# Output projection of a hybrid decoder layer: eight block products replaced by seven, with the operand sums made in the stage before

## The chip, the cores and the metric

The kernel runs on one core of one Trainium2 chip. The metric is the device time of one execution in microseconds (us). The kernel before took 1744.45 us, the median of three runs (1742.46 to 1744.65).

The core's engines work side by side: TensorE (PE in the profile; its weight loads are PEld) multiplies matrices, VectorE (DVE), ScalarE (ACT) and GpSimd (POOL) work elementwise, and SyncE's queue (SP) issues nearly all transfers between the main memory (DRAM) and the on-chip memory. Each engine takes its instructions in a fixed order and waits where an input is not there yet.

## The reference

One layer of a decoder for 1024 prompt tokens and 8 single sample tokens, in 32-bit floats, model width 1024. What matters here:

```python
x = x + jnp.concatenate([o_a, y], axis=-1) @ w['w_out']      # (tokens, 2048) @ (2048, 1024), plus the residual
h = rmsnorm(x, w['norm2_w'])
gate, val = jnp.split(h @ w['w_up'], 2, axis=-1)             # 1024 -> 2 x 2816
gate, buf_f_new = causal_dwconv(gate, buf_f, w['ffn_conv_w'], w['ffn_conv_b'])
x = x + (jax.nn.silu(gate) * val) @ w['w_down']
```

`o_a` (1024 wide) comes from eight heads of a gated recurrence (HGRN2), `y` (1024 wide) from the Mamba-2 mixer. Both are fed by one input projection. A final RMSNorm follows.

## The kernel before

All tokens (1032 with the samples) are processed together, with features on the 128 partitions and tokens along the free dimension. A product in 32-bit precision is made of three matmuls in the rounded format float32r: high x high, high x low and low x high. So every operand is first *split*: ACT casts it to its high part, DVE subtracts this from the original for the low part.

Order of the work:

- **Input projection and mixers** (to about 824 us). `in_job` makes one 128-wide output tile with 3 token chunks x 8 x 3 = 72 matmuls. The mixers' own work, `ssd` and `head(h)`, is interleaved by `drive`, which lets so many matmuls of the queue of jobs go by for each piece of the head. The heads' outputs and `y` are stored as 16 row tiles of 128 x 1032 in DRAM (`mix_d`; rows 0 to 7 from the heads, 8 to 15 from the mixer).
- **Output projection**, jobs a, b, c, d. The tokens are cut in two groups of 516 (`hf`), the inner dimension in the mixer's half (`r0 == 8`) and the heads' half (`r0 == 0`). a and b make the first group, c and d the second. Each of these has eight output tiles `m`, and each tile two column quarters of 258 tokens with 24 matmuls each. `mix_rows` loads eight row tiles of a half and splits them (L1107 to L1110). `Weight` loads 512 KB of `w_out` for a tile, and `round` splits it (L1093, L1094). Products of a and c are copied out of PSUM by ACT (L1166), those of b and d added by DVE (L1168). `residual` transposes a tile of the input x on TensorE (L852, L854) and adds it (L847). `final` stores the tile to `x1_d` (L1179) and collects squares for the norm (L1182 to L1186).
- **Token sets** `set_of(i)` for each group i: `norm` multiplies by the norm (L1326); then seven operands p1 to p7 of a seven-product block form are made of the four blocks a1, b1, a2, b2 (inner half 1 or 2, first or second 258 columns), by differences and sums (L1342, L1354), and split (L1336, L1337, L1355, L1358). The first group's set is made during c and d, the second group's during d and the first up group.
- **Up projection** in 22 groups `ups(j, seq)`. Each multiplies the seven token operands of both groups with seven weight operands: 14 x 12 = 168 matmuls of 258 columns. `up_sums` builds the weight sums on POOL (L1423), `up_split` splits them (L1444 to L1447). The down projection's weight sums are made ahead by `down_sums`, on POOL and by way of DRAM (`wsum_d`; L1203, L1206).
- **Down projection**, also as seven products, whose token operands (`at`) come back from DRAM (`act_d`). `last_step` starts its loads and splits in the last up group. `fin` makes the output.

What sets the order: the list of jobs, each with its run-ahead `load`; `after(n, f)`, which issues f after n more matmuls; `spread(pieces, n)`, which issues one piece every n matmuls; and for TensorE the order written by hand. On the other engines a planner orders the instructions by its estimates, bound by edges as in `behind` (an instruction of ACT goes behind the marked one).

The lines of the core loop and of the boundary to the up projection:

```python
hi, lo = mixes[r0, hf]
for c in cols:
    ps = psmm.tile([P, 512], F32, tag="mm", name=nm("mm"))[:, :QW]
    yield from steps(w.parts, 0, P, hi, lo, cs, ps)          # 8 rows x 3 matmuls
    ...
finish("d10")
after(22, lambda: set_norm(1, 1))
after(24, lambda: spread(second, 1))
for _ in ups(0, [(name, i) for i in range(2) for name in FIRST]):
    tick()
```

## Time and profile before

| | |
|---|---|
| median of the runs | 1744.45 us |
| the profiled execution, its own time | 1741.85 us |
| its span, first to last instruction | 1740.1 us |
| TensorE busy | 98% of the span |
| DVE, ACT, POOL busy | 68%, 48%, 29% |
| mean transfer rate | 138 GB/s |
| output projection, first to last matmul | 823.7 to 1045.0 us |
| up projection begins | 1045.0 us |
| down projection begins | 1496.7 us |

How to read it: a line of the profile names the source line, engine and operation, what it writes and reads, the shape and the count; after the bar stand the busy time in us, the mean of one in ns, and the idle time of the engine just before, with what ended it. Matmuls overlap, so their mean length is longer than the distance from one to the next.

### The profile page before, as it was taken

How to read it: one execution, taken by the hardware profiler on the slowest of the kernel's cores; microseconds unless marked ns; L12 is line 12 of the kernel's file. 1: busy time of each engine (PE TensorE's matmuls, PEld its weight loads, DVE VectorE, ACT ScalarE, POOL GpSimd, SP SyncE). 2: the span in 40 equal slices, each digit the busy share in tenths (PEclk: the TensorE clock that was granted, in tenths of full speed). 3: DMA queues.
4: the chain of work that ended last, by engine and by line, in shares of the span. 5: the costliest groups of instructions: out<-in, count | busy, mean ns of one | idle time of the engine just before them, and what ended most of it. 6: DMA issues, size and time to landing. Idle time of an engine off the chain costs nothing. (4 is left out here: it accounts for less than half of the span.)

```text
span 1740.1 us, 39019 instructions
## 1 busy us (share of the span) xinstructions
PE 1704.3 (98%) x15967; PEld 1650.9 (95%) x15967; DVE 1177.9 (68%) x2053; ACT 838.8 (48%) x1507; POOL 506.2 (29%) x500
## 2 busy tenths in 40 slices
PE   7999999999999999999999999999999999999998
PEld 7999998999999999999999998999999999999998
DVE  4657888568555654665666678877787777775664
ACT  6478688443543444444344444343433343444344
POOL 1102242112211210110112124776667775000001
PEclk9999999999999999999999999999999999999999
DMA  5123474564232322233556451445555543786463
GB/s 158 37 79 97 140 210 141 154 173 131 76 104 65 86 81 82 87 93 94 179 176 202 116 143 59 147 142 151 148 162 165 153 140 117 250 267 229 152 190 124
DMA packets 319689, 239.31 MB, mean 138 GB/s; under 512 B 18380, under 2 KB 287734, under 8 KB 319494
## 3 DMA queue, kind: packets, MB, share of 16 engines
q1 hardware_dynamic: 319222, 236.72, 45.4%
q8 instruction: 125, 2.05, 0.5%
q14 instruction: 54, 0.44, 0.1%
q0 software_dynamic: 288, 0.10, 0.0%
HBM read 178.18 MB, written 58.77 MB: 136 GB/s over the span
## 5 line engine op out<-in xcount | busy, mean ns | idle before, releaser
L94 PE MATMUL mm<-hh,wh 128*128 128x344 f32 x1248 | 406.4, 326 | 0.0
L94 PE MATMUL mm<-hl,wh 128*128 128x344 f32 x1248 | 403.7, 323 | 0.0
L94 PE MATMUL mm<-hh,wl 128*128 128x344 f32 x1248 | 402.4, 322 | 0.0
L94 PEld LDWEIGHTS mm<-hh,wh 128*128 128x128 f32 x1248 | 234.7, 188 | 2.9 <-issue 0.9
L94 PEld LDWEIGHTS mm<-hl,wh 128*128 128x128 f32 x1248 | 234.8, 188 | 2.2 <-issue 0.9
L94 PEld LDWEIGHTS mm<-hh,wl 128*128 128x128 f32 x1248 | 234.9, 188 | 2.0 <-issue 1.0
L94 PE MATMUL ub<-uh,wh 128*128 128x258 f32 x704 | 199.5, 283 | 2.1 <-DVE fext L1497 1.6
L94 PE MATMUL ub<-ul,wh 128*128 128x258 f32 x704 | 199.9, 284 | 1.5 <-DVE ul L1358 1.5
L94 PE MATMUL ub<-uh,wl 128*128 128x258 f32 x704 | 199.0, 283 | 0.0
L94 PE MATMUL mm<-mx,wh 128*128 128x258 f32 x1024 | 190.9, 286 | 1.6 <-DVE mx L1110 1.1
L94 PE MATMUL dn<-at,wh 128*128 128x260 f32 (+1 forms) x896 | 163.0, 282 | 0.0
L94 PEld LDWEIGHTS mm<-mx,wh 128*128 128x128 f32 x1024 | 158.5, 189 | 3.3 <-DVE mx L1110 1.6
L94 PE MATMUL ua<-uh,wh 128*128 128x258 f32 x528 | 150.1, 284 | 0.5 <-ACT us L1469 0.5
L94 PE MATMUL ua<-ul,wh 128*128 128x258 f32 x528 | 149.9, 284 | 0.0
L94 PE MATMUL ua<-uh,wl 128*128 128x258 f32 x528 | 149.4, 283 | 0.0
L94 PE MATMUL mm<-mx,wl 128*128 128x258 f32 x512 | 145.3, 284 | 1.7 <-DVE wl L1094 1.7
L94 PEld LDWEIGHTS dn<-at,wh 128*128 128x128 f32 x896 | 137.6, 188 | 0.0
L94 PEld LDWEIGHTS ub<-uh,wh 128*128 128x128 f32 x704 | 133.0, 189 | 2.5 <-ACT uh L1336 1.8
L94 PEld LDWEIGHTS ub<-ul,wh 128*128 128x128 f32 x704 | 133.4, 189 | 1.9 <-DVE ul L1358 1.9
L94 PEld LDWEIGHTS ub<-uh,wl 128*128 128x128 f32 x704 | 133.4, 190 | 0.0
L94 PE MATMUL dn<-at,wl 128*128 128x260 f32 (+1 forms) x448 | 126.6, 283 | 3.9 <-DVE wl L1613 3.9
L1447 DVE TENSOR_TENSOR wl<-wt,wh 128x512 fp32r<-128x512 f32 x88 | 89.5, 1036 | 58.3 <-ACT wh L1446 58.3
(342 smaller groups left out, 3726.9 us busy)
## 6 DMA issues: line engine op xcount, KB each, us to landing
ws<-in_w_in_dram SPq DMA_DIRECT2D x52, 512.0 KB
ws<-in_w_up_dram SPq DMA_DIRECT2D x44, 512.0 KB
at<-act_d SPq DMA_DIRECT2D x77, 258.0 KB
ws<-in_w_out_dram SPq DMA_DIRECT2D x36, 512.0 KB
wq<-in_w_down_dram SPq DMA_DIRECT2D x44, 256.0 KB
wsum_d<-wq SPq DMA_DIRECT2D x22, 512.0 KB
mx<-mix_d SPq DMA_DIRECT2D x32, 258.0 KB
csb<-cs_d SPq DMA_DIRECT2D x32, 256.0 KB
```

The lines of the kernel that those rows point to most:

```text
L94: PE.matmul(out, lhsT, rhs, start=start, stop=stop)
L1447: V.tensor_tensor(lo[:, cs], sums[name], hi[:, cs].bitcast(F32), op=ALU.subtract)
```

## The change

The output projection is written as a seven-product block form, too: the inner dimension has two halves (mixer, heads), the tokens of each group two column halves, and the output width two halves. With y0, y1 the mixer's rows and o0, o1 the heads' rows (first and second 258 columns of a group), the row operands are: p1 y0; p7 y0 - y1; p4 o1; p6 (y1 - o1) - y0; p5 y1 - o1; p2 o0; p3 o0 + p6.

- The jobs are p1, p7, p4, p6, p5, p2, p3. Each covers both token groups, has four output tiles (half the width) and 4 x 2 x 24 matmuls; p3 does group 0 for all four tiles and then group 1 with the same weights kept. Each needs its own eight row tiles.
- `row_sums`, new at the end of each head, loads the mixer's row tile (into the head's k buffer), makes the four sums on POOL and stores them to `row_d`; for the last head p7's row is not stored but subtracted on DVE when it is split.
- `out_sums` makes the weight sums for p6, p5, p4 and p7 from 16 groups on POOL and stores them to `wo_d`. It runs in the heads, ahead of the first four groups of `down_sums`, with one piece every 10 matmuls instead of every 70, and four pieces between a group's load and its sums.
- `out_add`: p1 and p7 are copied out of PSUM by ACT; p4, p6 and p5 are added or subtracted on DVE, with one more operation on POOL for p6 and p5; p2 and p3 are added on DVE. The second column halves are final after p5, the first after p2 (lower half of the width) and p3 (upper half).
- The residual is loaded in pieces of 258 tokens x 256 columns, two pieces ahead, and added during the products p6, p5 and p2.
- The token sets of both groups are made in two parts, `second_halves` (from p2 on) and `first_halves` (group 0 from p3b on, group 1 in the first up group). The norm's column multiplication goes to ACT, the multiplication by the row norm to DVE, on two tiles at once. DVE splits and set operations are now bound behind the last marked DVE eviction (`vbehind`).
- The first up group multiplies p5 and p4 of both groups first, then the other five of group 0 and of group 1.
- `last_step` opens and loads the first tiles of the down projection earlier and splits them in smaller pieces.

```diff
+    def residual_load(i, c, q):
+        t0, cols = (2 * i + c) * QW, slice(2 * q * P, (2 * q + 2) * P)
+        xs, xd = tl("t", "xs")[:, :512], tl("us", "xd")
+        if t0 + QW <= T:
+            fetch(xs.rearrange("p (b m) -> p b m", b=2), x_prompt[0, t0:t0 + 256, cols].rearrange("(b p) m -> p b m", p=P))
+            fetch(xd[:2, :256], x_prompt[0, t0 + 256:t0 + QW, cols])
         else:
+            n = T - t0 - P
+            fetch(xs[:, :256], x_prompt[0, t0:t0 + P, cols])
+            fetch(xs[:n, 256:], x_prompt[0, t0 + P:T, cols])
+            fetch(xd[:ND, :256], x_sample[:, 0, cols])
         return xs, xd
...
+    def residual(i, c, q, xs, xd):
+
+        n, nd = (P, 2) if (2 * i + c + 1) * QW <= T else (T - (2 * i + c) * QW - P, ND)
+        ps, pd = bank("xtp"), bank("xtd", "nx")
+        for m in range(2):
+            ms = slice(m * P, (m + 1) * P)
+            PE.transpose(ps[:, m * 256:m * 256 + P], xs[:, ms], ident)
+            PE.transpose(ps[:, m * 256 + P:m * 256 + P + n], xs[:n, 256 + m * P:256 + (m + 1) * P], ident[:n, :n])
+            PE.transpose(pd[:, m * 8:m * 8 + nd], xd[:nd, ms], ident[:nd, :nd])
...
+    def residuals(items):
+        loads = [residual_load(*it) for it in items[:2]]
+        for n, it in enumerate(items):
+            yield
+            if n + 2 < len(items):
+                loads.append(residual_load(*items[n + 2]))
+            residual(*it, *loads[n])
...
+        fetch(k[:, :NT], mix_d[8 + h])
...
+        spread(row_sums(h, k, sg), 14)
+
+    def halves(t):
+        return t.rearrange("p (i c t) -> p i c t", i=2, c=2)
+
+    ROWS = ("p7", "p5", "p6", "p3")
+    MID = 2 * QW
+    row_d = dram.tile([4, 8, P, MID], F32, name="row_d")
+
+    def row_sums(h, k, sg):
+        a, b = halves(k[:, :NT]), halves(sg[:, :NT])
+        yield
+        yield
+        G.tensor_tensor(b[:, :, 1], a[:, :, 1], b[:, :, 1], op=ALU.subtract)
+        G.tensor_tensor(a[:, :, 1], a[:, :, 0], a[:, :, 1], op=ALU.subtract)
+        G.tensor_tensor(a[:, :, 0], b[:, :, 1], a[:, :, 0], op=ALU.subtract)
+        G.tensor_tensor(b[:, :, 0], a[:, :, 0], b[:, :, 0], op=ALU.add)
+        yield
+        for n, t in enumerate((a[:, :, 1], b[:, :, 1], a[:, :, 0], b[:, :, 0])):
+            if n or h < H - 1:
+                SP.dma_start(row_d[n, h].rearrange("p (i t) -> p i t", i=2), t)
...
+    SUMS = ("p6", "p5", "p4", "p7")
+    rows, unsplit = {}, {}
+
+    def row_open(p):
+        rows[p] = [tl("hT", "mx", F32R) for _ in range(8)]
+        unsplit[p] = row_splits(p)
+
+    def row_load(p, rs):
+        for r in rs:
+            hi, lo = (t.bitcast(F32).rearrange("p (i t) -> p i t", i=2) for t in (rows[p][r][:, :MID], rows[p][r][:, MID:]))
+            if p in ROWS and (p, r) != ("p7", H - 1):
+                fetch(lo, row_d[ROWS.index(p), r].rearrange("p (i t) -> p i t", i=2))
+            else:
+                fetch(lo, halves(mix_d[r if p in ("p2", "p4") else 8 + r])[:, :, 1 if p == "p4" else 0])
+            if (p, r) == ("p7", H - 1):
+                fetch(hi, halves(mix_d[8 + r])[:, :, 1])
...
+    def out_src(p, m):
+        if p in SUMS:
+            return wo_d[m // 2, SUMS.index(p), m % 2]
+        r, c = {"p1": (8, 0), "p2": (0, 0), "p3": (0, 4)}[p]
+        return w_out[0, r * P:(r + 8) * P, (c + m) * P:(c + m + 1) * P].rearrange("(k p) m -> p k m", p=P)
+
+    def out_add(p, i, m, ps):
+        x_ = lambda h, c: xf(i, h, c)[:, m]
+        if p == "p1":
+            mark[0] = A.copy(x_(0, 0), ps)
+        elif p == "p7":
+            mark[0] = A.copy(x_(1, 1), ps)
+        elif p == "p4":
+            vmark[0] = V.tensor_tensor(x_(0, 1), x_(1, 1), ps, op=ALU.add)
+        elif p == "p6":
+            vmark[0] = V.tensor_tensor(x_(1, 0), x_(0, 0), ps, op=ALU.add)
+            G.tensor_tensor(x_(0, 1), x_(0, 1), x_(1, 0), op=ALU.add)
+        elif p == "p5":
+            vmark[0] = V.tensor_tensor(x_(1, 0), ps, x_(1, 0), op=ALU.subtract)
+            G.tensor_tensor(x_(1, 1), x_(1, 0), x_(1, 1), op=ALU.subtract)
+            final(i, 0, 1, m)
+            final(i, 1, 1, m)
+        else:
+            h = int(p == "p3")
+            vmark[0] = V.tensor_tensor(x_(h, 0), x_(h, 0), ps, op=ALU.add)
+            final(i, h, 0, m)
...
+    def out_sums():
+        return pair_sums(w_out[0].rearrange("(two i p) (gv h c) -> h i p two gv c", two=2, p=P, gv=2, h=2), wo_d, 1, range(2 * KT), 4)
...
-    job("conv", None, once(lambda: (spread(conv_states(), 60), spread(down_sums(range(2 * DK - GROUPS_UP)), 70))))
+    job("conv", None, once(lambda: (spread(conv_states(), 60), spread(chain(out_sums(), down_sums(range(2 * DK - GROUPS_UP), 4)), 10))))
...
+    OUT = ("p1", "p7", "p4", "p6", "p5", "p2", "p3")
+
+    def split_behind(n0, n, p):
+        after(n0, lambda: spread(unsplit[p], n))
+
+    def open_p1():
+        for key in ((0, 0, 0), (0, 1, 1), (1, 0, 0), (1, 1, 1)):
+            xtile(*key)
+        row_open("p1")
+        row_load("p1", range(8))
         for _ in range(4):
+            next(unsplit["p1"])
         mark[0] = heads[H - 1]["out"]
+        split_rest("p1")
+
+    def open_p7():
+        row_open("p7")
+        row_load("p7", range(8))
+        split_behind(12, 16, "p7")
+
+    def open_next(n):
+        p, nxt = OUT[n], OUT[n + 1]
+        split_rest(p)
+        row_open(nxt)
+        row_load(nxt, range(7 if nxt == "p4" else 8))
+        if nxt != "p4":
+            split_behind(60, 14, nxt)
+
+    begins = {("p1", 0): open_p1, ("p1", 1): open_p7}
+    for n in range(1, 6):
+        begins[OUT[n], 0] = lambda n=n: open_next(n)
+    for p in OUT[:6]:
+        for m in range(4):
+            out_job(f"{p}_{m}", p, m, begin=begins.get((p, m)), depth=4 if (p, m) == ("p2", 3) else 3)
+    for m in range(4):
+        out_job(f"p3a{m}", "p3", m, (0,), {0: lambda: split_rest("p3")}.get(m), True, "ttww"[m], 2, 4)
+    for m in range(4):
+        out_job(f"p3b{m}", "p3", m, (1,), depth=4 - m if m else 4)
...
-        drive(head(H - 1, heads[H - 1]), 32.0, "a5", 288)
+        drive(head(H - 1, heads[H - 1]), 32.0, "p7_1", 288)
+        row_load("p4", [7])
+        split_behind(10, 9, "p4")
+        finish("p7_3")
...
+    def second_halves(i):
+        b1, b2 = xf(i, 0, 1), xf(i, 1, 1)
+        yield from normed(i, 0, 1)
+        yield from normed(i, 1, 1)
+        sas[i] = quads(tl("xe", "sm")[:, :NT])
+        yield from comb(sas[i], b1, b2, ALU.subtract)
+        yield from put(i, "p4", b2, "big", "e" if i else "big")
+        while i and "p2_3" not in done:
+            yield
+        yield from put(i, "p5", sas[i], *(("hT", "hT") if i else ("e", "big")))
+
+    def first_halves(i):
+        a1, a2, b1, sa = xf(i, 0, 0), xf(i, 1, 0), xf(i, 0, 1), sas[i]
+        yield from normed(i, 0, 0)
+        yield from put(i, "p1", a1, "hT", "hT")
+        yield from comb(sa, sa, a1, ALU.subtract)
+        yield from comb(b1, a1, b1, ALU.subtract)
+        yield from put(i, "p6", sa, "hT", "hT")
+        yield from put(i, "p7", b1, "hT", "big")
+        yield from normed(i, 1, 0)
+        yield from comb(sa, sa, a2, ALU.add)
+        yield from put(i, "p2", a2, "hT", "big")
+        yield from put(i, "p3", sa, "hT", "big")
...
-    FIRST = ("p1", "p2", "p4", "p5", "p6", "p7", "p3")
+    FIRST = ("p5", "p4", "p1", "p6", "p7", "p2", "p3")
...
     def last_step(n):
+        if n == 3:
+            tok_open(0)
+            tok_load(0, range(5))
         if n == 5:
             unit_load(0)
-            tok_open(0)
         if n == 6:
-            tok_load(0, range(8))
+            tok_load(0, range(5, 8))
+        if n == 8:
+            tok_load(0, range(8, 9))
+            tok_split(0, range(0, 3))
         if n == 9:
             unit_split(0)
-            tok_load(0, range(8, 10))
-            tok_split(0, range(0, 4))
+        if n == 10:
+            tok_split(0, range(3, 7))
         if n == 11:
-            tok_load(0, range(10, 11))
             unit_load(1)
-            tok_split(0, range(4, 8))
         if n == 12:
-            tok_split(0, range(8, 11))
+            tok_load(0, range(9, 11))
+            tok_split(0, range(7, 9))
         if n == 13:
             unit_split(1, 1)
+            tok_split(0, range(9, 11))
...
+        finish("p4_1")
+        late = residuals([(i, 1, q) for q in range(4) for i in range(2)])
+        next(late)
+        finish("p4_3")
+        after(4, lambda: spread(late, 20))
+        finish("p6_2")
+        late2 = residuals([(i, 0, q) for q in range(2) for i in range(2)])
+        next(late2)
+        finish("p6_3")
+        for _ in late:
+            pass
+        after(8, lambda: spread(late2, 36))
+        finish("p5_2")
+        late3 = residuals([(i, 0, q) for q in range(2, 4) for i in range(2)])
+        next(late3)
+        finish("p5_3")
+        for _ in late2:
+            pass
         up_load(0)
+        after(4, lambda: spread(late3, 36))
+        after(36, lambda: set_norm(0, 1))
+        after(50, lambda: set_norm(1, 1))
+        sets = chain(second_halves(0), second_halves(1))
+        after(56, lambda: spread(sets, 9))
+        finish("p2_3")
+        for _ in late3:
+            pass
+        up_sums(0)
+        finish("p3a3")
+        after(22, lambda: set_norm(0, 0))
+        sets0 = first_halves(0)
+        after(26, lambda: spread(sets0, 3))
+        for m in range(3):
+            finish(f"p3b{m}")
+            after(3, lambda m=m: up_split(0, m))
+        finish("p3b3")
+        for _ in chain(sets, sets0):
+            pass
+        up_split(0, 3)
         after(20, lambda: set_norm(1, 0))
+        after(24, lambda: spread(first_halves(1), 3))
+        for _ in ups(0, [(name, i) for names in (FIRST[:2], FIRST[2:]) for i in range(2) for name in names]):
```

337 lines of the change are left out of this document (101 added, 236 removed).

## The prediction

> **What bounds the kernel now.** I read the page first, then the chain of waits in order of time, then the busy time of each engine by stretches.
>
> ```profile
> span 1740.1 us, 39019 instructions
> PE 1704.3 (98%) x15967; PEld 1650.9 (95%) x15967; DVE 1177.9 (68%) x2053; ACT 838.8 (48%) x1507; POOL 506.2 (29%) x500
> ...
> L94 PE MATMUL mm<-mx,wh 128*128 128x258 f32 x1024 | 190.9, 286 | 1.6 <-DVE mx L1110 1.1
> ...
> L94 PE MATMUL mm<-mx,wl 128*128 128x258 f32 x512 | 145.3, 284 | 1.7 <-DVE wl L1094 1.7
> ```
>
> TensorE sets the time: 1704.3 of 1740.1 us. The output projection is the 1024 + 512 = 1536 matmuls that read mx. Their 284 ns are latencies that overlap; the price is the spacing in the chain (start, length, what):
>
> ```profile
> 961.55 0.44 PE xtp L852 x4
> 961.98 0.15 PE xtd L854
> ...
> 1022.24 0.45 PE n2ms L94 x2
> ...
> 1076.53 5.77 PE ub L94 x48
> ```
>
> 48 matmuls of 258 columns take 5.77 us, 120.3 ns each. A residual tile's four transposes take 0.44 us, the small fifth one 0.15. One norm matmul (two records) costs 0.45.
>
> Where TensorE is not fed, by stretches (length, then busy us and count of each engine, clock, DMA share, GB/s):
>
> ```profile
> 430.00:820.00 390.00, 389.48 (x4972) 371.25 (x4972) 220.72 (x398) 172.09 (x267) 62.66 (x52) 1.00 0.30 85
> 823.66:875.00 51.34, 49.21 (x782) 45.79 (x781) 35.71 (x64) 20.51 (x40) 8.52 (x6) 1.00 0.50 152
> 940.00:960.00 20.00, 20.00 (x162) 19.50 (x162) 16.04 (x25) 8.11 (x16) 4.65 (x6) 1.00 0.80 240
> 991.50:1045.05 53.55, 51.48 (x416) 50.15 (x416) 39.24 (x58) 27.57 (x44) 15.01 (x14) 1.00 0.49 140
> 1045.05:1074.80 29.75, 25.73 (x183) 24.70 (x182) 27.34 (x47) 12.58 (x25) 13.53 (x13) 0.89 0.06 19
> 1540.00:1560.00 20.00, 20.00 (x172) 19.75 (x171) 17.13 (x36) 10.15 (x16) 0.00 (x0) 1.00 0.88 280
> ```
>
> The heads (430 to 820) lose 0.5 us. The last product of the projection (991.5 to 1045) loses 53.55 - 51.48 = 2.1. The first up group loses most: 183 records, 2 of them a norm, are 181 x 0.1203 + 0.45 = 22.2 us of work in 29.75, a loss of 7.5, while DVE is busy 27.34 of 29.75 us, 92%. So the bound changes hands there: DVE normalizes, combines and splits the token sets that the up projection reads. Start and spacing of the matmuls show it:
>
> ```profile
> 1066.61 0.58 PE L94 MATMUL ub<-ul,wh 128*128 128x258 f32 x1 [1.33 <-DVE ul L1358]
> 1066.99 0.42 PE L94 MATMUL ub<-uh,wl 128*128 128x258 f32 x1
> ...
> 1072.15 0.42 PE L94 MATMUL ua<-uh,wl 128*128 128x258 f32 x1
> ```
>
> After a wait of 1.33 us, the last of several (29.75 - 25.73 = 4.0 us of idleness in all), 25 matmuls start between 1066.99 and 1072.15, 0.215 us apart and not 0.12: the granted clock fell (0.89 in the mean of the stretch).
>
> **The change, part by part.** Durations come from the profiled execution, 1741.85 us (span 1740.1 and 1.75 around it); the median of the runs shown is 1744.45, and differences are applied to that.
>
> *Products.* Seven products of 4 x 2 x 24 = 192 matmuls are 1344 instead of 1536: 192 x 0.1203 = **-23.1 us**, all on the path.
>
> *Transposes and norms on TensorE.* The residual has 64 large transposes as before and 32 small ones instead of 16: 16 x 0.15 = **+2.4**. The two first-half norms add three matmuls each instead of one, 8 in all instead of 4: 4 x 0.45 = **+1.8**.
>
> *The tail on DVE.* Before, the first token group's set was made during products c and d. Now nothing is final before p5 (second column halves) and p2 and p3 (first halves), so all 60 set operations of both groups come after p2 starts. DVE prices:
>
> ```profile
> L1094 DVE TENSOR_TENSOR wl<-ws,wh 128x1024 fp32r<-128x1024 f32 x35 | 45.1, 1288 | 17.7 <-ACT wh L1093 17.1
> ...
> L1168 DVE TENSOR_TENSOR x<-x,mm 128x258 f32<-128x258 f32 x32 | 13.4, 418 | 13.1 <-PE mm L94 13.1
> ...
> L1337 DVE TENSOR_TENSOR ul<-x,uh 128x516 fp32r<-128x516 f32 x12 | 8.2, 714 | 1.9 <-ACT uh L1336 1.8
> ...
> L1447 DVE TENSOR_TENSOR wl<-ws,wh 128x512 fp32r<-128x512 f32 x5 | 3.3, 680 | 0.0
> ```
>
> From the start of p2 to the end of the first up group DVE has: 60 set operations and 8 row splits of 128x516, 68 x 0.714 = 48.6; seven weight splits, 9.0; 26 evictions (8 of p2, 8 of p3, 10 up), 10.9; four residual tiles at 0.68 (512 wide), 2.7; four norms of three operations at 0.418 (258 wide), 5.0; thirteen 512-wide up splits, 8.8. Sum 85.0 us. TensorE has 192 + 192 + 168 = 552 matmuls, 66.4, four residual tiles at 0.74, 3.0, and eight norm matmuls, 3.6: 73.0 us. DVE is over by 12.0 us, so it becomes the bound of this stretch. How well can it be kept busy? The nearest rows are 92% (1045 to 1075) and 39.24 of 53.55, 73% (991 to 1045, where TensorE still led). A stretch in which DVE leads is like the first: 85.0 / 0.92 = 92.4 us, a loss of 19.4, against 2.1 + 7.5 = 9.6 now: **+9.8**. Bounds: 85.0 us with DVE never idle, +2.4; at 73%, 116.4 us, +33.8. The up group's new order (p5 and p4 of both groups first) is in this: it gives the first halves 48 matmuls, 5.8 us, of cover. Queued behind the waiting splits are the up weights' splits and, on ACT, the casts and squares in between.
>
> [...]
>
> *The start.* While head 7 finishes, p7's eight row splits (8 x 0.714 = 5.7) replace some five residual tiles (3.4) in the first half of a stretch in which DVE is busy 35.71 of 51.34 us and 2.1 us are lost. **+1**, bounds 0 and +3. Waiting here are the head's scalings of q and k, and TensorE for them.
>
> *The heads.* Sixteen weight groups add 64 POOL adds, eight heads add 32 row sums:
>
> ```profile
> L1203 POOL TENSOR_TENSOR wq<-wq 128x256 f32<-128x256 f32 x16 | 13.2, 822 | 117.7 <-DMA wq<-in_w_down_dram 86.2 <-DVE SS L1012 30.6
> ...
> L1342 POOL TENSOR_TENSOR sm<-x 128x516 f32<-128x516 f32 x4 | 5.4, 1356 | 12.5 <-DVE x L1326 12.5
> ...
> L1447 DVE TENSOR_TENSOR wl<-wt,wh 128x512 fp32r<-128x512 f32 x88 | 89.5, 1036 | 58.3 <-ACT wh L1446 58.3
> ```
>
> 64 x 0.822 + 32 x 1.356 = 96 us of POOL, whose queue is busy 62.66 of 390 us: **0**, hidden by the input projection's matmuls (389.48 of 390). If the cover failed: a DVE split takes 1036 ns where POOL works most of the time (L1447 from wt) against 680 where it does not, so 96 us of POOL add up to 33 us to DVE's 220.72 of 390; a fifth of that reaching TensorE is 6. Bounds 0 and +6. The tiles k and sg of a head live longer, until their sums are stored; the next user of such a buffer is the v of the head after next, half a head later. New on SP's queue in the heads: 8 loads of 516 KB, 31 stores of sums, 32 half loads and 16 stores of weights.
>
> [...]
>
> *Transfers.* Sizes:
>
> ```profile
> ws<-in_w_out_dram SPq DMA_DIRECT2D x36, 512.0 KB
> ...
> mx<-mix_d SPq DMA_DIRECT2D x32, 258.0 KB
> ```
>
> Row loads rise from 32 to 57, weights fall from 36 to 28. The worst product is p5: 8 x 258 KB rows, 4 x 512 KB weights, 16 x 129 KB stores (128 x 258 words) and about three 256 KB residual tiles are 6.9 MB in 26 us, 266 GB/s, where the highest 20 us seen carry 280. At 240, the highest of the projection, it would take 28.8 us. **+1**, bounds 0 and +6 (p5 and p2). Late next would be the rows of the following product.
>
> *Up to down.* The first token tiles of the down projection are opened and loaded two to three products earlier, past the last act stores on SP, and split in five pieces:
>
> ```profile
> PE dn L94 <- DVE wl L1613: 3.9, 3, 1.7
> ```
>
> The wait is for down weights, which stand behind those loads. **-1**, bounds -3.9 and +3.9. The first up weights' two 512 KB loads move from behind c3 to behind p5_3, their POOL sums to behind p2; their splits still come a product later: 0.
>
> Sum: -23.1 + 2.4 + 1.8 + 9.8 + 1 + 0 + 1 - 1 = **-8.1**, so 1744.45 - 8.1 = **1736** (profiled: span about 1732).
>
> **The rivals.**
> *The tail is covered.* If the order lets DVE's splits hide so that the loss stays at today's 9.6, the +9.8 goes: -17.9, **1726.5**. For it: p2 and p3a have slack at their starts. Against it: 85.0 us do not fit in 73.0, and even a DVE that never idles gives 1729; below that, set work must start before p2.
> *The tail starves: slower.* The splits are queued behind evictions, and each cast on ACT sits among squares that wait for evictions. Place: p2 to the end of the first up group. The change loses everything when the loss reaches 9.6 + 17.9 = 27.5 us, a stretch of 100.5, that is DVE at 85%. At 79% it is 107.6, a loss of 34.6 and a sum of -17.9 + 25.0 = +7.1: **1751.5**; at 73%, 1760. [...] Against: when DVE led, 92%.
> *Transfers decide.* +6 in place of +1, and no gain at the down projection: -2.1, **1742**. For it: 266 against 280 GB/s. Against: the rows have a product's time to land. The same time holds if the "well ahead" sums are not there in time, which would stop p7.
> *The heads pay* the 6 us of POOL and DVE: -2.1, **1742**. Against it: 389.48 of 390.
>
> **How the numbers follow.** Forecast 43% (own range 1728 to 1740.5), tail covered 19%, tail starves 20%, transfers 14%, heads 4%. A measurement of this kernel tells 0.2%, 3.5 us, from no change. Forecast and covered tail are faster: 62%. Transfers and heads are mostly no change: 17%. The starving tail and the rest are slower: 21%. The range runs from inside the covered tail (1720: 6.5 of today's 9.6 us gone too) to inside the starving one: 1720 to 1755, leaving out about 15%.
>
> **What would show it.** 1344 matmuls on mx with spacing 0.12; 32 small and 64 large residual transposes; the stretch from p2 to the end of the first up group near 92 us with DVE at about 92%; no new gap in the heads; a down start that loses 3 us or less. It is wrong if that stretch is under 86 us or over 100, or if TensorE waits for rows or sums in p7 to p5.

## The result: 52 us slower, and the profile after

The changed kernel took **1796.06 us**, the median of four runs (1790.54 to 1798.97), against 1744.18 of the kernel before: a ratio of 1.0296, with a 95% interval from 1.0269 to 1.0322. The forecast was 1736 with a range up to 1755. The profiled execution took 1790.54 us; its span is 48.7 us longer than that of before, and this is what is divided up below.

From the page of the changed kernel (the last line is a group of instructions, with its busy us, mean ns, and the idle us ahead of it):

```profile
span 1788.8 us, 39058 instructions
PE 1704.3 (95%) x15799; PEld 1644.4 (92%) x15799; DVE 1241.8 (69%) x2079; ACT 849.8 (48%) x1544; POOL 639.0 (36%) x604
...
L94 PE MATMUL mm<-mx,wh 128*128 128x258 f32 x896 | 173.6, 292 | 8.3 <-ACT wh L1138 3.2
```

The 192 matmuls are gone (896 + 448 = 1344 on mx; the second number is the group with wl), yet TensorE's busy time is the same 1704.3 us: slower matmuls (granted clock 0.986 in the mean, 0.996 before) took back what was saved, and the 48.7 us are idle time of TensorE on top. POOL works 133 us more. Where the 48.7 us lie is read from stretches that hold the same work in both kernels (length, busy us and count of PE, PEld, DVE, ACT, POOL, clock, DMA share, GB/s). First before, then after:

```profile
430.00:823.70 393.70, 393.18 (x4997) 374.88 (x4996) 224.42 (x404) 174.83 (x270) 62.98 (x53) 1.00 0.30 85
823.70:895.40 71.70, 69.57 (x945) 65.43 (x943) 50.93 (x88) 30.81 (x59) 11.32 (x8) 1.00 0.48 146
895.40:994.90 99.50, 99.50 (x813) 97.88 (x812) 59.33 (x88) 42.37 (x75) 16.89 (x21) 1.00 0.62 184
994.90:1073.00 78.10, 72.44 (x559) 70.47 (x559) 63.03 (x97) 36.31 (x62) 27.14 (x25) 0.96 0.33 95
```

```profile
430.00:855.10 425.10, 400.80 (x4993) 380.97 (x4991) 259.77 (x397) 173.78 (x269) 166.89 (x141) 0.98 0.48 141
855.10:928.90 73.80, 65.32 (x902) 62.64 (x903) 58.81 (x83) 34.65 (x65) 22.84 (x16) 0.95 0.55 174
928.90:958.80 29.90, 26.23 (x195) 25.73 (x194) 14.35 (x21) 8.85 (x13) 1.42 (x1) 0.89 0.66 217
958.80:1019.30 60.50, 59.43 (x459) 54.82 (x458) 35.32 (x63) 21.90 (x37) 20.39 (x25) 1.00 0.69 213
1019.30:1122.20 102.90, 81.47 (x598) 76.43 (x597) 86.40 (x133) 56.67 (x116) 39.99 (x31) 0.92 0.29 91
```

| stretch | before | after | measured | forecast |
|---|---|---|---|---|
| heads, 430 us to the first matmul on mx | 393.7 | 425.1 | **+31.4** | 0 |
| first 384 matmuls on mx, with the end of head 7 (p1, p7) | 71.7 | 73.8 | +2.1 | -3.7 |
| next 768 before, 576 after (p4, p6, p5) | 99.5 | 90.4 | -9.1 | -17.9 |
| last 384 and the first up group (p2, p3) | 78.1 | 102.9 | **+24.8** | +14.6 |
| the other up groups, then down | 667.1 | 666.6 | -0.5 | -1 |

The forecast's column is its own terms put into these stretches, with its own prices of a residual tile, 0.59 us before and 0.74 after. The tiles have moved: eight of the sixteen stood in the second row before and none does now, the third row has twelve in place of eight, the fourth four in place of none. So the second row is 1 - 8 x 0.59, the third -23.1 + 12 x 0.74 - 8 x 0.59 + 1, the fourth 9.8 + 1.8 + 4 x 0.74. TensorE's largest new waits in the changed kernel (total, number, longest; the first was 2.0 us before, the others were not there):

```profile
PE a L94 <- DVE q L944: 20.4, 11, 5.9
PE o L94 <- DVE SS L1030: 6.4, 2, 3.5
PE n2ms L94 <- POOL n2r L1254: 6.4, 1, 6.4
...
PE n2ms L94 <- ACT n2sq L1247: 5.9, 1, 5.9
```

The first is the scan of the heads (a are its masked products, q its scaled queries; 6.7 of the 20.4 us fall in p1, where head 7 ends), the second the states of the sample tokens in the heads, the other two the norm in the first up group.

### The profile page after: what moved, and what is told of

The parts are those of the page before. It is cut to its first block, busy times and chain, and to the rows that moved or that the text cites. A ratio compares the mean times of both kernels' runs of the same rounds, so it can differ in the third digit from the quotient of the medians.

```text
span 1788.8 us, 39058 instructions
## 1 busy us (share of the span) xinstructions
PE 1704.3 (95%) x15799; PEld 1644.4 (92%) x15799; DVE 1241.8 (69%) x2079; ACT 849.8 (48%) x1544; POOL 639.0 (36%) x604
## 4 chain that ended last, share of the span: by engine, by line
PE 57%; DVE 9%; DMA 3%; issue 2%; ACT 1%; SPq 0%; DVEq 0%; POOL 0%; ACTq 0%
PE mm L94 16%; PE ub L94 14%; PE dn L94 11%; PE ua L94 10%; PE a L94 2%; DVE tt L946 2%; PE o L94 1%; DVE u L1401 1%; DVE k L943 1%; DVE wl L1139 1%; DMA xs<-in_x_prompt_dram 1%; DVE q L944 1%; DMA mx<-row_d 1%; DMA Sh<-in_state_hgrn_dram 1%; PE kv L94 0%
## 5 line engine op out<-in xcount | busy, mean ns | idle before, releaser
L94 PE MATMUL ub<-u,wh 128*128 128x258 f32 x1408 | 256.9, 283 | 0.2 <-DVE us L1506 0.2
L94 PEld LDWEIGHTS ub<-u,wh 128*128 128x128 f32 x1408 | 218.7, 190 | 0.6 <-DVE us L1506 0.4
L94 PE MATMUL ub<-u,wl 128*128 128x258 f32 x704 | 199.8, 284 | 0.0
L94 PE MATMUL ua<-u,wh 128*128 128x258 f32 x1056 | 192.5, 283 | 2.0 <-DVE val L1537 1.5
L94 PE MATMUL mm<-mx,wh 128*128 128x258 f32 x896 | 173.6, 292 | 8.3 <-ACT wh L1138 3.2
L94 PEld LDWEIGHTS ua<-u,wh 128*128 128x128 f32 x1056 | 163.1, 189 | 2.4 <-DVE val L1537 1.7
L1269 POOL TENSOR_TENSOR wq<-wq 128x256 f32<-128x256 f32 x80 | 77.4, 967 | 232.4 <-DMA wq<-in_w_out_dram 149.3
L94 PE MATMUL ua<-u,wl 128*128 128x258 f32 x528 | 149.1, 282 | 0.0
L94 PEld LDWEIGHTS ub<-u,wl 128*128 128x128 f32 x704 | 133.7, 190 | 0.1
L94 PEld LDWEIGHTS ua<-u,wl 128*128 128x128 f32 x528 | 99.8, 189 | 0.0
```

The lines of the kernel that those rows point to most:

```text
L94: PE.matmul(out, lhsT, rhs, start=start, stop=stop)
L1269: G.tensor_tensor(out, x_, y_, op=ALU.add)
```

## The experiments

Times are medians; ratios are against the kernel before, timed on the same chip alongside. "First mx" is the start of the projection in the profile, 823.7 before and 855.1 after. It comes from one execution each: the eight profiles here whose heads hold the work of before put it between 823.2 and 831.7, so a few us between two kernels mean nothing.

### The heads: which of the additions costs 31 us

Four kernels take parts of the additions out. h_noadds leaves out the 64 weight adds and the 32 row-sum adds and keeps all loads and stores:

```diff
-        G.tensor_tensor(b[:, :, 1], a[:, :, 1], b[:, :, 1], op=ALU.subtract)
-        G.tensor_tensor(a[:, :, 1], a[:, :, 0], a[:, :, 1], op=ALU.subtract)
-        G.tensor_tensor(a[:, :, 0], b[:, :, 1], a[:, :, 0], op=ALU.subtract)
-        G.tensor_tensor(b[:, :, 0], a[:, :, 0], b[:, :, 0], op=ALU.add)
...
+                if first:
+                    pass
+                elif subbed[0] is None:
```

h_norow leaves out the row sums with their transfers (the first three edits below), h_nowsum the weight sums with theirs (the last two), h_none both; the products then read plain rows and weights:

```diff
-        fetch(k[:, :NT], mix_d[8 + h])
...
-        spread(row_sums(h, k, sg), 14)
...
-                fetch(lo, row_d[ROWS.index(p), r].rearrange("p (i t) -> p i t", i=2))
+                fetch(lo, halves(mix_d[r if p in ("p5", "p3") else 8 + r])[:, :, 1 if p in ("p7", "p5") else 0])
...
-            return wo_d[m // 2, SUMS.index(p), m % 2]
...
-    job("conv", None, once(lambda: (spread(conv_states(), 60), spread(chain(out_sums(), down_sums(range(2 * DK - GROUPS_UP), 4)), 10))))
+    job("conv", None, once(lambda: (spread(conv_states(), 60), spread(down_sums(range(2 * DK - GROUPS_UP), 1), 70))))
```

> The 64 weight-sum adds and the 32 row-sum adds on POOL in the heads are left out; their loads and stores stay, so the sums hold raw rows. The changed kernel took 1796, 52 us more than before; its first output-projection matmul starts at 855 us and not at 824, so the heads cost 31 us. Theory POOL (its adds stretch and delay DVE's two-input operations): the start goes back to about 826 to 832 and the time to about 1768 to 1774. Theory queue (the extra transfers on SP hold up the loads of the sample states): the start stays above 845 and the time above 1786.

> The heads of the kernel before: no row sums, no weight sums, and none of their transfers; the projection reads plain rows and plain weight blocks in their place. Start of the projection at 824 to 826 by every theory; the time is then the cost of the new projection and its tail alone: 1744 + 18 = 1762 to 1766 if the heads and the tail add up, and near 1740 if the late heads were also what starves the tail.

> Only the row sums of the heads (32 POOL adds, 8 loads of 516 KB, 31 stores) are left out; the weight sums stay. If the row sums at each head's end delay the next head's sample states, the start falls to about 835; if the weight sums, spread over all heads, are the cause, it stays near 850. Time 1776 in the first case, 1790 in the second.

> Only the weight sums (64 POOL adds, 32 loads of 256 KB, 16 stores of 512 KB in the heads) are left out; the row sums stay and the early down-projection sums run at the spacing of before. If the weight sums are the cause, the start falls to about 835 and the time to 1776; if the row sums are, they stay near 850 and 1790.

| | time | ratio (95%) | first mx |
|---|---|---|---|
| h_noadds | 1755.25 | 1.0057 (1.0040 to 1.0074) | 824.9 |
| h_none | 1757.21 | 1.0066 (1.0040 to 1.0092) | 825.7 |
| h_norow | 1759.72 | 1.0077 (1.0051 to 1.0103) | 827.8 |
| h_nowsum | 1786.93 | 1.0237 (1.0214 to 1.0260) | 852.0 |

The heads of h_noadds:

```profile
430.00:824.90 394.90, 394.38 (x5004) 376.06 (x5004) 223.09 (x403) 174.62 (x270) 64.64 (x52) 1.00 0.53 154
```

The transfers by themselves cost nothing that can be measured: with all of them (154 GB/s in place of 85) and no adds the projection starts at 824.9, and h_none is no faster. The 64 weight adds cost 2.5 us without the row sums (1759.72 - 1757.21, within the noise) and 9.1 beside them (1796.06 - 1786.93). The 32 row sums, some 43 us of POOL, cost the rest. How, the timeline of one head shows. Before, and then h_nowsum, on VectorE (start, length, what; x6 are six products one after another, of 256, 128, ... 8 columns):

```profile
519.15 1.65 DVE L927 TENSOR_TENSOR tt<-tt 128x256 f32<-128x256 f32 x6
```

```profile
523.74 5.96 DVE L946 TENSOR_TENSOR tt<-tt 128x256 f32<-128x256 f32 x6
```

And what POOL does in h_nowsum at that time, and then TensorE:

```profile
521.15 2.00 POOL L1089 TENSOR_TENSOR sg<-k,sg 128x516 f32<-128x516 f32 x1 [3.32 <-DMA mix_d<-sg]
...
525.99 1.30 POOL L1092 TENSOR_TENSOR sg<-k,sg 128x516 f32<-128x516 f32 x1
527.25 1.03 POOL L924 TENSOR_TENSOR vb<-vb,k 128x512 f32<-128x512 f32 x1
```

```profile
531.89 0.75 PE L94 MATMUL a<-q,k 128*32 128x32 f32 x64 [2.99 <-DVE q L944]
```

Six short products that took 1.65 us take 5.96. In the kernel before they are 0.42 to 0.17 us long; here they are 1.21, 1.07, 1.27, 0.93, 0.17 and 1.12. Three of them meet a row sum, and two meet the products for the sample tokens (L924, L926) that stand behind the sums on POOL; each of the five ends within 0.3 us of the end of POOL's operation. They are a chain, the scan's decays, and the first products on TensorE hang on it. In h_nowsum the chain is longer in all six heads ahead of the projection, by 26 us together, of the 28 us that the projection starts later. The sums start there because the store of the head's output, which reads the tile that they overwrite, has just landed.

In the changed kernel the picture is less even. The chain takes 5.97 us in two of the six heads; in the others it takes 1.65 to 2.73, the sums start near its end, and what they meet are the products of the scan's levels (L943 and L944, 0.90 and 0.92 us in the mean of 36 each, against 0.80 and 0.76 before). And TensorE's 6.4 us at o come by another way: the store of a weight sum stands ahead of the sample states' loads on SP's queue and waits for its adds on POOL (SP, then VectorE, which waits for those states):

```profile
495.56 0.39 SPq L193 DMA_DIRECT2D wo_d<-wq  x1
496.05 1.81 SPq L193 DMA_DIRECT2D Sh<-in_state_hgrn_dram  x2
```

```profile
500.09 0.69 DVE L925 TENSOR_TENSOR Sh<-Sh,f 128x512 f32<-128x512 f32 x1 [6.66 <-DMA Sh<-in_state_hgrn_dram]
```

Neither h_noadds nor h_nowsum has this wait of TensorE.

That the row sums' loss comes of their running time and not of their waits or their place in POOL's queue was tested with sums of 8 columns and with copies of 516:

```diff
-        G.tensor_tensor(b[:, :, 1], a[:, :, 1], b[:, :, 1], op=ALU.subtract)
+        G.tensor_tensor(b[:, :, 1, :4], a[:, :, 1, :4], b[:, :, 1, :4], op=ALU.subtract)
...
```

```diff
-        G.tensor_tensor(b[:, :, 1], a[:, :, 1], b[:, :, 1], op=ALU.subtract)
+        G.tensor_copy(b[:, :, 1], a[:, :, 1])
...
```

The first is r_tiny, the second r_copy.

> The 32 row-sum operations on POOL stay at their places, with their waits and the stores behind them, but work on 8 columns each (two blocks of 4) and not on 516, so the rows that the projection reads are mostly unsummed. If the loss in the heads is the running time of these operations beside the scan (some 43 us of POOL in all, 27 us of kernel time), it goes: the projection starts near 828 us and not 855, the time is about 1769 (1796 - 27). If it is their waits, their place in POOL's order ahead of the decode products, or their stores, nothing is gained: 1793 to 1797.

> The 32 row-sum operations on POOL are replaced by copies of the same 516 columns at the same places (one operand less; the rows that the projection reads are unsummed). If any POOL work of this length beside the scan slows VectorE, the loss stays in proportion to POOL's busy time: 27 us at the adds' length, 14 at half. If it is the second operand that collides, the heads lose under 5 us and the time is 1769 to 1774.

r_tiny took 1769.53 us (1.0134, 1.0105 to 1.0164), first mx 832.3: all but 0.5 of the 27 us expected are gone from the time, as the theory of the running time had it. r_copy took 1764.45 (1.0109, 1.0081 to 1.0136), first mx 831.9. The smallest of the six products (busy us, mean ns) after, in r_tiny and in r_copy; before it has 168 ns:

```profile
L946 DVE TENSOR_TENSOR tt<-tt 128x8 f32<-128x8 f32 x5 | 3.7, 748 | 0.2
```

```profile
L946 DVE TENSOR_TENSOR tt<-tt 128x8 f32<-128x8 f32 x5 | 0.9, 176 | 0.2
```

```profile
L946 DVE TENSOR_TENSOR tt<-tt 128x8 f32<-128x8 f32 x5 | 2.2, 450 | 0.2
```

So a copy collides as well (450 against 176 ns), and the theory that the second operand alone does it falls. Its projection starts no later than with the tiny sums, though. The copies are shorter (0.6 to 1.0 us); that what is left of the delay fits in the slack of the chain was not shown. The loss is not in proportion to POOL's time.

### The same sums on VectorE

r_dve issues the four sums on VectorE one at a time, 27 to 54 matmuls into the next head:

```diff
-        G.tensor_tensor(b[:, :, 1], a[:, :, 1], b[:, :, 1], op=ALU.subtract)
+        V.tensor_tensor(b[:, :, 1], a[:, :, 1], b[:, :, 1], op=ALU.subtract)
+        yield
...
```

r_dve2 issues them from 72 matmuls on, but for the last two heads:

```diff
+        for _ in range(3 if h >= H - 2 else 9):
+            yield
```

r_dve3 issues them from 84 matmuls on, again but for the last two heads, and ties each behind the scan's latest mask copy:

```diff
+            with behind_scan(V):
+                V.tensor_tensor(out, x_, y_, op=op)
```

> The four row sums of each head run on VectorE, one at a time about 27 to 54 matmuls into the next head; the output is the whole computation. On VectorE an add of 516 columns is 0.69 us (a row of before), 8 x 4 x 0.69 = 22 us, in heads where VectorE was busy 220.72 of 390 us. Theory of the POOL overlap: the heads lose 3 to 8 us and not 31 (each add stands once in the scan's chain), time 1769 to 1776. Rival, that any sum inside the scan costs its length: loss 22 or more, time 1787 or more.

> The row sums of the heads on VectorE as in the run before, but 72 matmul steps into the next head and not 27 (the last two heads keep 27, since the projection needs their rows soon). The output is the whole computation. At 27 the sums stood in front of the scan's first products on VectorE and waited up to 6.1 us for the store of the head's output; that kernel took 1796.8 us. At 72 the scan has VectorE waiting for TensorE at every level (2.2 to 2.4 us each). Theory that only the crowded start of the scan is hurt: 20 us or more of the 31 come back, 1770 to 1777. Rival, that a sum costs its length wherever it stands in the scan: 1788 or more.

> The row sums on VectorE, now held in VectorE's own order behind the scan's mask copies (in the two runs before, the order of VectorE's instructions had them first at about 7 us into the head wherever they were issued). The output is the whole computation. They stand now between the second and fourth scan levels, where VectorE waits 2.2 to 2.4 us for TensorE at every level, except in the last two heads. Theory that only a sum in the crowded first 15 us of a head costs time: at least 20 of the 31 us come back, 1768 to 1777. Rival, that the scan's chain pays every sum by its length (22 us): 1785 or more.

r_dve took 1796.81 us (1.0295, 1.0265 to 1.0326), r_dve2 1795.21 (1.0289, 1.0274 to 1.0304): nothing gained, and the rival seemed right. But the trace of r_dve2 shows its first sum where that of r_dve had stood, ahead of the scan's first product (L974), and stalled there for a store:

```profile
525.08 0.70 DVE L1092 TENSOR_TENSOR sg<-k,sg 128x516 f32<-128x516 f32 x1 [2.50 <-DMA mix_d<-sg]
525.69 1.22 DVE L974 TENSOR_TENSOR q<-q,f 128x1024 f32<-128x1024 f32 x1
```

```profile
DVE sg L1092 <- DMA mix_d<-sg: 20.6, 5, 6.2
```

Issuing an instruction later does not move it: the planner orders VectorE by its own estimates, in which the store was done. r_dve2 had not tested what it was meant to. In r_dve3 the sums are tied behind the mask copies of the scan:

```profile
527.41 0.45 DVE L985 COPY_PREDICATED amc<-mlow,a 128x256 f32<-128x256 uint8 x1
527.75 1.45 DVE L1093 TENSOR_TENSOR sg<-k,sg 128x516 f32<-128x516 f32 x1
```

It took 1775.46 us (1.0165, 1.0134 to 1.0196), first mx 842.2: 20.6 us less than the changed kernel, for the whole computation. The place decides, not the length: this sum is no shorter (1.45 us, against 0.70 above). Of the 31 us at the start of the projection 18 remain here, and 12 and 22 in the two kernels below that have the same sums.

### The first up group: is VectorE the bound

Both kernels start from h_none, 1757.21 us, whose stretch from the first up matmul to the first down matmul (1048.4 to 1512.6) is 464.2 us against 451.7 before.

t_late has the first of these edits, t_nocomb the second (in `first_halves` alone):

```diff
-        after(20, lambda: set_norm(1, 0))
-        after(24, lambda: spread(first_halves(1), 3))
+        after(46, lambda: set_norm(1, 0))
+        after(50, lambda: spread(first_halves(1), 3))
```

```diff
-            vbehind(lambda: V.tensor_tensor(t[:, q], x_[:, q], y_[:, q], op=op))
+            vbehind(lambda: V.tensor_tensor(t[:, q, :4], x_[:, q, :4], y_[:, q, :4], op=op))
```

> With the heads, rows and weights of the kernel before (no sums taken in the heads; so the last products read plain rows and weights), the norm matmuls of the second token half's first block are issued 46 instead of 20 matmuls into the first up group, and the sets that follow them at 50 instead of 24. Without this edit the same kernel took 1757.2 us. Theory that TensorE's order costs the first up group its waits of 5.9 and 6.4 us with the slower clock behind each: 10 to 17 us gained, 1740 to 1747. Rival, that VectorE's own work sets the end of the group: it does the same work in the same order and the waits only move behind the 46 matmuls, 0 to 4 us gained, 1753 to 1757.

> As the kernel that took 1757.2 us (heads of before, no sums), with the twelve sums and differences of token halves in the first halves' sets cut from 516 to 8 columns on VectorE; waits and order stay, and the sets that the up projection reads are partly uncombined. Twelve operations of 0.69 to 1.09 us shrink to about 0.17: 7 to 9 us less on VectorE between the last product and the end of the first up group. Theory that VectorE sets the end there: 6 to 9 us gained, 1748 to 1751. Rival, that TensorE's order of the norm matmuls or the squares set it: under 3 us gained, 1754 to 1757.

t_late took 1758.03 us (1.0076, 1.0054 to 1.0097), and the stretch is 464.2 us again. TensorE's waits only moved:

```profile
1063.21 1.23 PE L94 MATMUL n2ms<-n2r,ones 128*128 128x258 f32 x2 [3.23 <-POOL n2r L1250]
...
1089.17 0.39 PE L94 MATMUL ub<-u,wh 128*128 128x258 f32 x1 [2.75 <-DVE u L1397]
```

t_nocomb took 1750.19 (1.0038, 1.0023 to 1.0052), the stretch 457.0: the twelve operations, 0.69 us before and 0.16 here, are 6.3 us less on VectorE, and the kernel takes 7 us less. VectorE is the bound there. The edit also ends TensorE's wait of 6.4 us for POOL's add of the squares (n2r); but t_late halves that wait (3.23) and gains nothing, so it is not what binds.

In the changed kernel VectorE's own order makes the wait. The evictions of the last product (L1213) stand behind set work, and the squares and the norm hang on them. Its timeline:

```profile
1091.87 0.42 DVE L1213 TENSOR_TENSOR x<-x,mm 128x258 f32<-128x258 f32 x1
...
1096.36 3.43 DVE L1401 TENSOR_TENSOR u<-sm,u 128x516 fp32r<-128x516 f32 x2
1099.71 0.41 DVE L1213 TENSOR_TENSOR x<-x,mm 128x258 f32<-128x258 f32 x1
```

The last matmul on mx is at 1083.6, the last eviction 16 us later. Four of the operations between them take 1.7 us and not 0.68: POOL makes the second up group's weight sums from 1092.51 to 1099.24.

### The projection itself

Three kernels, again from h_none, go after the wait of TensorE on head 7's scan in p1.

p_mend loads the first six rows of p7 in `open_p1`, behind p1's, and puts a residual tile's four large transposes ahead of the two small ones:

```diff
+        row_open("p7")
+        row_load("p7", range(6))
...
-            PE.transpose(ps[:, m * 256:m * 256 + P], xs[:, ms], ident)
+            PE.transpose(ps[:, m * 256:m * 256 + P], xs[:, m * P:(m + 1) * P], ident)
+        for m in range(2):
             PE.transpose(ps[:, m * 256 + P:m * 256 + P + n], xs[:n, 256 + m * P:256 + (m + 1) * P], ident[:n, :n])
-            PE.transpose(pd[:, m * 8:m * 8 + nd], xd[:nd, ms], ident[:nd, :nd])
+        for m in range(2):
+            PE.transpose(pd[:, m * 8:m * 8 + nd], xd[:nd, m * P:(m + 1) * P], ident[:nd, :nd])
```

p_mend2 loads all eight rows there; p_mend3 also ties the splits of p7's rows, and the difference that makes its last row, behind the scan's mask copies:

```diff
-        row_load("p7", range(6))
+        row_load("p7", range(8))
```

```diff
+            if p == "p7":
+                with behind_scan(V):
+                    V.tensor_tensor(lo, x_, hi.bitcast(F32), op=ALU.subtract)
```

> The heads of before, no sums, plain rows and weights (as the kernel that took 1757.2 us), and two edits of the projection: the first six rows of product p7 are loaded right after p1's, ahead of head 7's state stores on the DMA queue, and a residual tile's four large transposes stand together ahead of its two small ones. Theory: the wait of 7.0 us on the scan in p1 goes with the slow clock behind it (9 us), and a residual tile falls from 0.99 to 0.74 us (16 x 0.25 = 4 us): 1742 to 1747. If the wait in p1 is set by head 7's own chain, p1 stays near 44 us and the time is 1752 to 1755.

> As the kernel that took 1752.9 us (heads of before, no sums, p7's first six rows ahead, transposes grouped), with the last two rows of p7 loaded ahead of head 7's state stores too. In that kernel the last row's difference waited 4.87 us for its load and held VectorE in front of the scan, and TensorE waited 5.0 us and ran 25 matmuls at 0.2 us each. Theory: both go, 1744 to 1748. Rival: p1 stays near 44 us, 1751 to 1754.

> As the kernel that took 1751.8 us (heads of before, no sums, all eight rows of p7 loaded ahead of head 7's state stores, transposes grouped), with the splits of p7's rows and the last row's difference held on VectorE behind the scan's mask copies, one between two levels. In that kernel the difference stood ahead of the scan's first level and waited 4.50 us for its row; TensorE waited 5.89. Theory that the wait in p1 is VectorE's order and not the transfers: it goes, p1 falls from 42.9 to 35-37 us, 1743 to 1747. Rival, that p1 is bound by head 7's chain: p1 stays at 41 or more, 1750 to 1753.

They took 1752.92 us (1.0047, 1.0028 to 1.0065), 1751.76 (1.0041, 1.0027 to 1.0056) and 1749.34 (1.0029, 1.0017 to 1.0040). In the timeline of h_none, then in that of p_mend2, VectorE waits in p1 for a row of p7 with the scan behind it:

```profile
846.99 0.70 DVE L1169 TENSOR_TENSOR mx<-mx 128x516 fp32r<-128x516 f32 x1 [6.50 <-ACT mx L1168]
...
849.03 1.08 PE L94 MATMUL a<-q,k 128*32 128x32 f32 x64 [7.04 <-DVE q L944]
```

```profile
837.43 1.47 DVE L1164 TENSOR_TENSOR dif<-mx 128x516 f32<-128x516 f32 x1 [4.50 <-DMA mx<-mix_d]
```

Loading the rows earlier moved the split forward by as much, and the wait stayed: 5.89 us of TensorE in p_mend2. Held behind the scan, it fell to 1.53, and p1 from 43.1 to 40.1 us, less than half of what was expected. So the wait comes of VectorE's order, which puts an operation that still waits for a transfer ahead of the scan; an earlier load alone does not end it. The kernel before has 71.7 us for the first 384 matmuls, with the end of head 7, and p_mend3 69.7. But eight residual tiles are in the 71.7, some 8 x 0.78 = 6.2 us of TensorE (below), and none in the 69.7: about 4 us of loss are left in p1, and their cause is open.

p_mend left p1 as it was (44.1 us); its projection is 2.2 us shorter than h_none's by the residual. A tile's transposes in TensorE's timeline, five in the kernel before, then six in the changed kernel and in p_mend:

```profile
961.39 0.60 PE L852 MATMUL xtp<-ident,xs 128*128 128x128 f32 x4
...
962.07 0.39 PE L94 MATMUL mm<-mx,wh 128*128 128x258 f32 x1
```

```profile
970.74 0.27 PE L851 MATMUL xtp<-ident,xs 128*128 128x128 f32 x1
...
971.05 0.22 PE L853 MATMUL xtd<-ident,xd 8*128 8x8 f32 x1
...
971.73 0.39 PE L94 MATMUL mm<-mx,wl 128*128 128x258 f32 x1
```

```profile
945.73 0.38 PE L850 MATMUL xtp<-ident,xs 128*128 128x128 f32 x2
...
946.25 0.28 PE L854 MATMUL xtd<-ident,xd 8*128 8x8 f32 x2
946.47 0.51 PE L94 MATMUL mm<-mx,wh 128*128 128x258 f32 x2
```

From the first transpose to the next matmul are 0.68 us before, 0.99 where large and small ones alternate, and 0.74 with like ones together. (With the matmuls on both sides, which also come a little later, a tile costs 0.10 us more, 0.78 before.) Of the 4 us that this is worth in 16 tiles, TensorE's waits for residual rows (0.9 us in h_none, 3.0 in p_mend) took half back.

### The parts that could be mended, in one kernel, and the one part that seemed to gain

These four join edits that stand above. all_mend has r_dve2's sums, and p_mend's rows and transposes; all3 has r_dve3's sums, p_mend's transposes, and p7's rows ahead but for the seventh, which needs head 6's sums; all4 is all3 with p_mend3's tied splits. b_last is the kernel before with the change's `last_step` alone:

```diff
+        if n == 3:
+            tok_open(0)
+            tok_load(0, range(5))
...
-            tok_load(0, range(8))
+            tok_load(0, range(5, 8))
+        if n == 8:
+            tok_load(0, range(8, 9))
+            tok_split(0, range(0, 3))
...
```

> The whole computation with the three edits on the changed kernel: row sums on VectorE at 72 steps, p7's rows loaded ahead, transposes grouped. If the gains add up: 1796 - 22 (heads) - 9 (p1) - 4 (transposes) = 1761, 1757 to 1766. If the row sums only move their loss: 1778 or more. The kernel before is not reached either way, since weight sums (3 us) and the tail (20 us against 10 before) stay.

> The whole computation with the held row sums, p7's rows ahead of head 7's state stores (the seventh, which needs head 6's sums, stays where it was), and the grouped transposes. If the parts add: 1796 - 22 (heads) - 6 (p1) - 4 (transposes) = 1764, 1758 to 1770. If the held sums bring nothing: 1780 or more.

> The whole computation: row sums held behind the scan, p7's rows loaded ahead and their splits held too, transposes grouped. The same without the held splits took 1767.4 us with 40.5 us for p1. If p1 falls to 35-37 us: 1761 to 1765. Not below the kernel before in any case.

> The kernel before with only the change's new last step of the up phase (the first down product's tokens opened, loaded and split in other steps). In the changed kernel the wait of the first down matmuls on their weights was 1.5 us and not 3.9, and from the down start to the end it took 241.4 and not 243.4 us. If that part is worth the same by itself: 2 us faster, 1741.5 to 1743.5, ratio 0.999. If the wait was set by what stands ahead of it and only moves: no change.

all_mend took 1786.92 us (1.0235, 1.0211 to 1.0259), its sums not having moved; all3 1767.36 (1.0129, 1.0104 to 1.0155); all4 **1764.23** (1.0110, 1.0085 to 1.0135), all for the whole computation. 32 of the 52 us come back, 20 stay. In all4 the heads lose 12.3 us (first mx 836.0), the projection takes 217.4 us against 221.3 before, and from the up start to the down start 464.3 against 451.7. So even then the seven products gain 4 us where they stand, and from the up start to the down start 12.6 are lost.

b_last took 1744.59 us, 1.000 (0.9987 to 1.0013): by itself the new last step does nothing that can be measured. No version beat the kernel before.

## Why the prediction was wrong, step by step

- **Heads: 0, "hidden by the input projection's matmuls", at most +6.** This is the step that failed, with +31.4. Its own pieces were nearly right: 32 x 1.356 = 43 us of row sums, and "up to 33 us" added to VectorE, where the stretches above have 259.77 - 224.42 = 35. What failed is "a fifth of that reaching TensorE": nearly as much did, 23.8 us as waits and 7.6 as slower matmuls (TensorE busy 400.80 against 393.18 us, granted clock 0.98), because the sums run just beside the stretch of a head in which TensorE's next products hang on VectorE's chain. That TensorE was busy 389.48 of 390 us was an average over stretches with different limits. The rival "the heads pay" had the mechanism, with 6 us and a chance of 4%. Not foreseen at all were the 6.4 us behind the weight sums' stores. In the heads of the changed kernel the product of 8 columns took 748 ns in the mean, 168 before, beside sums of 1.39 to 1.50 us (means of L1089 to L1092).
- **Products: -23.1.** Right in count; in the stretch p4 to p5 they are diluted to -9.1 by the next two points and by four more residual tiles.
- **Transposes: +2.4.** Mis-sized. A tile takes 0.99 us and not 0.74, since small and large transposes alternate, and before it took 0.68 by the same measure, not 0.59: 16 x (0.99 - 0.68) = +5.0. The price came from a row in which four large ones stand together.
- **Transfers: +1, 0 to +6.** Two things. p4 lost 6.8 us (29.9 against 192 x 0.1203 = 23.1), a little over the bound, and the prediction's warning, "if TensorE waits for rows or sums in p7 to p5", came true. In the changed kernel ACT's waits in p4 and p6, and the timeline of SP's queue:

```profile
ACT mx L1170 <- DMA mx<-row_d: 11.8, 4, 9.9
```

```profile
930.35 0.51 SPq L1096 DMA_DIRECT2D row_d<-sg  x1
...
932.35 5.97 SPq L193 DMA_DIRECT2D mx<-row_d  x8
```

  ACT waited 9.9 us for rows of p6, a weight's cast stood behind it, and TensorE waited 3.20 us for the cast. Bandwidth was not the cause: h_noadds, with all transfers and no adds, has p4 at 23.1 us. On SP's queue p6's loads stand behind the stores of head 7's row sums, which wait for POOL. The sums' length is the smaller part of it: with sums of 8 columns (r_tiny) p4 still takes 27.6 us, and there, too, POOL's first sum waits 3.4 us for the store of the head's output. With the sums on VectorE it takes 23.8 to 24.2. In p6 a residual load cost another 1.1 us.
- **The start: +1, 0 to +3.** Also mis-sized. The stretch grew by 2.1 us although eight residual tiles, 6.2 us, had left it, so the loss is some 8 us. The mechanism named, row splits in front of the scan, is what h_none shows (73.4 us, with a wait of 7.04). In the changed kernel the largest wait of p1, 5.95 us, has another cause: head 7's chain meets head 6's row sums, as in the heads:

```profile
865.63 5.99 DVE L946 TENSOR_TENSOR tt<-tt 128x256 f32<-128x256 f32 x6
```

```profile
874.04 1.09 PE L94 MATMUL a<-q,k 128*32 128x32 f32 x64 [5.95 <-DVE q L944]
```

- **The tail on DVE: +9.8, with norms and transposes +14.6.** The mechanism is right, t_nocomb shows it, and the work nearly: 85.0 us were forecast, 86.40 measured, of which some 4 are four operations stretched by POOL (below). The utilization was mis-sized: 86.40 of 102.90 us is 84%, not 92%, and the stretch is 102.9, not 92.4. By stretches of the changed kernel, columns as above:

```profile
1019.30:1045.00 25.70, 23.57 (x179) 21.47 (x178) 19.18 (x34) 15.15 (x30) 7.03 (x8) 1.00 0.61 196
...
1065.00:1083.70 18.70, 18.21 (x141) 17.84 (x141) 12.43 (x20) 8.98 (x19) 3.74 (x4) 0.96 0.25 75
1083.70:1100.00 16.30, 4.63 (x26) 3.50 (x24) 16.30 (x22) 7.49 (x15) 13.86 (x7) 0.70 0.05 16
```

  VectorE is idle for 6.5 and 6.3 us of the first two stretches, while the last products run, and then, from the start of the up group, busy without a gap while TensorE does 4.63 us of work in 16.3. This is the rival "the tail starves", which put the point of no gain at a stretch of 100.5. What it did not name is POOL, whose weight sums stretched four of VectorE's operations here from 0.68 to some 1.7 us.
- **Up to down: -1.** 241.4 against 243.4 in the profiles, but b_last shows no gain, so the 2 us may be chance.
- **Weight sums "well ahead".** Right: p7, which needs them first, takes 29.6 us in the changed kernel and in h_none, which has no sums.
- **The clock.** The forecast put the slow matmuls of the first up group behind a wait of 1.33 us, the last of several. A longer one, 1.59 us, ended at 1064.21; the granted clock was 0.81 from there to 1066.60 and 0.50 in the 4 us from 1066.61, after the wait of 1.33. In p3 of the changed kernel it was 1.00 in the 4 us after waits of 0.88 and 0.96 us, and 0.59 after one of 3.19. Which waits lower it was not tested.

With the heads as before and no sums at all (h_none) the change is still 0.66% slower: 222.7 us of projection against 221.3, and 12.5 us more from the up start to the down start. Even without the failed step the forecast would have missed by 21 us, by the tail (p2 to the end of the first up group took 104.5 us, 12 over its term) and the start (5) above all.

**Open.** Why 12 to 22 us of the heads' loss stay with the sums tied on VectorE was not tested; the weight sums are in it, and the last two heads' sums are still issued early. That the tail could be mended by another order of evictions and sets was not tried; t_late shows only that TensorE's order does not.

## What to carry to other kernels

POOL's idle time was no room here for sums beside VectorE's chain of short products, 1.65 us without them and 5.96 with them in h_nowsum. So look at what such a chain does in the stretch where the new work becomes ready, since the planner started it there, and do not price a short operation at its own length alone where it meets a long one: the product of 8 columns took 748 ns and not 168. Moving the call that issues an instruction moves nothing where a planner sets the order; tie it to an instruction, and read in the trace where it stands before concluding anything. Matmuls saved at TensorE's price buy nothing where the work that is left on VectorE is longer than the matmuls beside it: 86.40 us against 81.47 from p2 to the end of the first up group of the changed kernel. And before calling a stretch unchanged, count what has moved out of it.

## What the runs showed of the hardware

Which of the two engines was slowed changed within one stretch. In the first up group of the changed kernel a POOL add of 258 columns, 0.76 us in the median of its line, took 7.10 us beside VectorE's stream of two-operand operations of 0.69 us:

```profile
1085.45 7.10 POOL L1254 TENSOR_TENSOR n2r<-n2r,n2sq 128x258 f32<-128x258 f32 x1 [8.10 <-ACT n2sq L1253]
```

It ended 0.7 us after VectorE had come to an eviction (L1213 at 1091.87); from then on POOL's adds followed one another, and four of VectorE's operations took some 1.7 us each. What let it end there was not tested. TensorE's wait of 6.4 us for this add stands in h_none and all4 as well, and not in t_nocomb, whose stream was cut short. So POOL's add was slow through ten of VectorE's operations, and then four of VectorE's were slow through POOL's sums. And a wait cost more than itself: after TensorE's wait of 3.19 us in p3 of the changed kernel, the matmuls from 1063.44 to 1066.02 were 0.215 us apart and not 0.12, some 1.1 us more, at a granted clock of 0.51 from 1063.06 to 1066.40:

```profile
1063.06 0.58 PE L94 MATMUL mm<-mx,wl 128*128 128x258 f32 x1 [3.19 <-DVE wl L1139]
```
